# Attention of a second block on Trainium2: logits with keys on the rows instead of transposed probabilities

## The chip, the cores and the metric

The kernel runs on one core of a Trainium2 chip. The metric is the device time of one execution in microseconds. TensorE does the matrix products, VectorE (DVE), ScalarE (ACT) and GpSimd (POOL) the rest; SyncE (SP) issues the DMAs.

## The reference, cut to what matters

Two transformer blocks run one after the other on 512 tokens of width 1024. The second has two layers. Each layer projects its input, mixes it in three ways (a Fourier mix, an attention, a gated recurrence called hgrn), multiplies the joined result by `w_out` and ends with a feed-forward. The change concerns this attention: 8 query heads share 2 key heads, the width of a head is 64, and 512 image queries see 256 context keys and 512 image keys. In the first layer 256 context queries see the context keys alone.

```python
def attend(q, k, v):
    s = jnp.einsum('bkgqd,bksd->bkgqs', q, k).astype(jnp.float32) * (HEAD_DIM ** -0.5)
    p = jax.nn.softmax(s, axis=-1).astype(v.dtype)
    return jnp.einsum('bkgqs,bksd->bkgqd', p, v)
```

## The kernel before, in words

All activations lie with features on the 128 rows and tokens along the columns, in buffers called slots of 128 x 512 numbers. Products that need more than one pass are split: a number is held as a rounded part and a remainder, both of type fp32r, which TensorE takes in one pass; plain fp32 takes more. Weights come in raw buffers of 512 KB and are split by ScalarE and VectorE.

Nothing is ordered by hand. Each piece of work is a generator that yields instructions, requests for buffers, or waits for a result (`Fut`). A planner (`Sched`) holds a clock for each engine, gives each instruction a cost (`mmcost` for matmuls), and always emits the instruction that can start earliest; equal ones go by a task's priority. The order found becomes the order of each engine's queue. Some orders are given: `ORDER2` names the order in which the projections of an image layer run: i (values of the recurrence), kv, hq (queries of the recurrence), q0 and q1 (attention queries of pairs 0, 1 and 2, 3), fo (Fourier), g (gate). The first blocks of each layer are four gates of the recurrence. The context stream of the first layer uses `ORDER2C` and runs beside block 1's feed-forward.

The attention works in pairs of heads, one of either key head: `att2_pair`, four pairs a stream. `stack_q` turns the queries (`turned`) and lays the rounded part and the remainder on the two halves of the 128 rows; `stack_k` does it for the keys. Then each tile of 128 queries runs by itself: `att2_head` makes the logits with queries on the rows, takes the maximum along the columns, the exponential with its sum, divides, and transposes the probabilities by TensorE; `att2_tile` multiplies them by the values, in fp32, with the two heads on the two halves of TensorE's columns. The recurrence (`hgrn`) makes many small products on 64 rows and 32 or 64 columns, each followed by VectorE, GpSimd or ScalarE, and its products cannot start before hq. `out_proj` multiplies the joined result by `w_out` in three parts: part 0 takes three of the eight row blocks (Fourier and pair 0) for the first 256 tokens, part 1 the other five for the same tokens (`OUT2`), part 2 all eight for the last 256 tokens.

PSUM is split by kind: two banks `psm` for the dense products, two `psx` for all else, and two double banks `psd` for logits and the recurrence's small products. When no `psm` is free, a task may take a `psx` instead.

Of the kernel before, what the change touches and what calls it, by code (L numbers as in the profile page):

```python
# [9 lines left out]
F = mybir.dt.float32  # L10
R = mybir.dt.float32r
# [13 lines left out]
HALF = (slice(0, 256), slice(256, 512))  # L25

# [123 lines left out]
ORDER2 = ("i", "kv", "hq", "q0", "fo", "q1", "g")  # L150
# [101 lines left out]
class Alloc:  # L252


    __slots__ = ("kind", "dt", "n")

    def __init__(s, kind, dt=F, n=1):
        s.kind, s.dt, s.n = kind, dt, n
# [177 lines left out]
class Sched:  # L436
# [127 lines left out]
    def run(s):  # L564
        while s.tasks:
            best = None
            progress = False
            for t in list(s.tasks):
                while t.pend is not None:
# [7 lines left out]
                    if isinstance(p, Alloc):  # L577
# [3 lines left out]
                        if len(s.freel[kind]) < p.n + ahead + (ROOM.get(t.name.rstrip("0123456789"), 0) if kind == "slot" else 0):  # L581
                            kind = s.SPARE.get(kind)
# [41 lines left out]
class Kernel:  # L624
    def __init__(s, ctx, tc, A, out, dbg=None):
# [8 lines left out]
            "sm": (sb, [P, 8]), "pr": (sb, [P, 768]), "psm": (pp, [P, T]), "psx": (pp, [P, T]), "psd": (pp, [P, 2 * T]),  # L634
            "tka": (None, None), "tko": (None, None),
        }, {"slot": SLOTS, "raw": 4, "rawc": 2, "wu": 3, "at": 2, "sm": 24, "pr": 4, "psm": 2, "psx": 2, "psd": 2, "tka": 3, "tko": 2})
# [138 lines left out]
    def stack_q(s, q, n, turn=False):  # L775
# [7 lines left out]
        if turn:  # L783
            q = yield from s.turned(q, n)
# [10 lines left out]
    def stack_k(s, kf, n, fut, turn=False):  # L795

        k = yield kf
# [7 lines left out]
        for h in range(2):  # L805
            hi, lo = t[2 * h], t[2 * h + 1]
            own, other = (slice(0, 64), slice(64, P)) if h == 0 else (slice(64, P), slice(0, 64))
# [3 lines left out]
            yield DMA(lo[other].bitcast(F), lo[own].bitcast(F))  # L811
# [1147 lines left out]
    def att2_head(s, i, q, keys, h, fut):  # L1959
        m = yield Alloc("sm")  # L1960
        w = sum(wk for _, wk in keys)
        S = yield Alloc("psd")
        c, mms = 0, []
        for K, wk in keys:
            for j in range(2):
                mms.append((S[:, c:c + wk], q[h][:, i * P:(i + 1) * P], K[h][j], j == 0, j == 1))
            c += wk
        yield PE(*mms)
        yield V("tensor_reduce", m[:, 0:1], S[:, :w], mybir.AxisListType.X, ALU.max, negate=True)
        pr = yield Alloc("pr")  # L1970
        yield ACT("activation", pr[:, :w], S[:, :w], AF.Exp, bias=m[:, 0:1], accum_out=m[:, 1:2])
        s.free(S)
        yield V("reciprocal", m[:, 2:3], m[:, 1:2])
        yield alt(V("tensor_scalar", pr[:, :w], pr[:, :w], m[:, 2:3], None, ALU.mult),
                  G("tensor_tensor", pr[:, :w], pr[:, :w], m[:, 2:3].to_broadcast([P, w]), ALU.mult))
        s.free(m)
        pts = []
        for c0 in range(0, w, T):
            ww = min(T, w - c0)
            pt = yield from s.ps()  # L1980
            yield PE(*[("T", pt[:, c * P:(c + 1) * P], pr[:, c0 + c * P:c0 + (c + 1) * P], s.c["ident"])
                       for c in range(ww // P)])
            t = yield from s.slot(T if ww > TC else TC)
            yield copy_any(t[:, :ww], pt[:, :ww])
            s.free(pt)
            pts += [(t, c) for c in range(ww // P)]
        s.free(pr)
        fut.set(pts)

    def att2_tile(s, i, q, keys, vals, mix, done):  # L1990

        fs = [Fut(), Fut()]
        for h in range(2):
            s.spawn(s.att2_head(i, q, keys, h, fs[h]), 1, "att2h")
        pts = yield from gather(fs)
        mms = []
        nt = len(vals)
        o = yield from s.ps()
        for c in range(nt):
            for h in range(2):  # L2000
                t, cc = pts[h][c]
                mms.append((o[64 * h:64 * h + 64, :P], vals[c][:, 64 * h:64 * h + 64],
                            t[:, cc * P:(cc + 1) * P], c == 0, c == nt - 1, (0, 64 * h)))
        yield PE(*mms)
        for h in range(2):
            s.free(*[t for t, c in pts[h] if c == 0])
        yield from s.split_into(mix, i, o[:, :P])
        s.free(o)
        done.set()

    def att2_pair(s, qf, nq, keysf, valsf, fut, futh=None):
        tok = yield Alloc("tko")
        q0 = yield qf
        q = yield from s.stack_q(q0, nq, True)
# [7 lines left out]
        o = yield from s.pair_mix(nq)  # L2022
        dones = []
        for i in range(nq // P):
            d = Fut()
            dones.append(d)

            def run(i=i, d=d):
                tk = yield Alloc("tka")
                yield from s.att2_tile(i, q, keys, vals, o, d)  # L2030
                s.free(tk)

            s.spawn(run(), 1 + i // 2 * LATE, f"att2_{i}")
        for i, d in enumerate(dones):
            yield d
            if futh is not None and i % 2:
                futh[i // 2].set(o)
        s.free_stack(*q)
        s.free(tok)
        fut.set(o)  # L2040
# [502 lines left out]
    def layer(s, L, adaf, cs=None):  # L2543
# [186 lines left out]
SLOTS = 65  # L2730
# [26 lines left out]
```

## Time and profile before

| | us |
|---|---|
| median of 3 runs | 2281.55 (2280.36 to 2285.49) |
| the profiled execution | 2282.2 |
| its span, first to last instruction | 2280.1 |

A row of the profile holds times in microseconds, or nanoseconds where it says so. PE is TensorE's matmuls, PEld its weight loads, which overlap them. The lengths of matmuls overlap too, since a matmul's record lasts until its last result is out; how fast TensorE works is read from start to start. A plain fp32 matmul stands in the trace as two records. A granted clock of 1.00 is 2.4 GHz.

### The profile page before, as it was taken

How to read it: one execution, taken by the hardware profiler on the slowest of the kernel's cores; microseconds unless marked ns; L12 is line 12 of the kernel's file. 1: busy time of each engine (PE TensorE's matmuls, PEld its weight loads, DVE VectorE, ACT ScalarE, POOL GpSimd, SP SyncE). 2: the span in 40 equal slices, each digit the busy share in tenths (PEclk: the TensorE clock that was granted, in tenths of full speed). 3: DMA queues.
4: the chain of work that ended last, by engine and by line, in shares of the span. 5: the costliest groups of instructions: out<-in, count | busy, mean ns of one | idle time of the engine just before them, and what ended most of it. 6: DMA issues, size and time to landing. Idle time of an engine off the chain costs nothing.

```text
span 2280.1 us, 42611 instructions
## 1 busy us (share of the span) xinstructions
PE 2222.6 (97%) x17065; PEld 1930.2 (85%) x17065; DVE 1559.9 (68%) x3665; ACT 918.6 (40%) x1679; POOL 214.3 (9%) x286
## 2 busy tenths in 40 slices
PE   8999999999999989999999999999989999999998
PEld 6877987888887978799888888889978889888887
DVE  6878877797888678798765433556768776444445
ACT  5455645442224436664212111124536655222223
POOL 0010014110000061110000000000153100000000
PEclk9999999999999989999999999999999999999999
DMA  5455444434444611234433212333221223222223
GB/s 185 145 152 171 167 155 131 144 130 162 147 153 150 199 61 48 93 115 146 148 128 123 102 65 86 126 130 125 105 80 39 75 74 131 93 101 93 99 96 111
DMA packets 92118, 272.72 MB, mean 120 GB/s; under 512 B 10944, under 2 KB 20952, under 8 KB 91920
## 3 DMA queue, kind: packets, MB, share of 16 engines
q1 hardware_dynamic: 91920, 269.99, 35.4%
q8 instruction: 135, 2.21, 0.4%
q14 instruction: 63, 0.52, 0.1%
HBM read 253.66 MB, written 7.38 MB: 114 GB/s over the span
## 4 chain that ended last, share of the span: by engine, by line
PE 87%; DVE 8%; ACT 2%; issue 2%; DMA 1%; POOL 0%; SPq 0%; DVEq 0%; ACTq 0%; POOLq 0%
PE psm L543 67%; PE psx L543 17%; DVE slot L543 6%; PE psd L543 3%; DVE wu L543 2%; ACT slot L543 1%; ACT wu L543 1%; POOL slot L543 0%; DVE sm L543 0%; DMA raw<-w1in 0%; DMA slot<-ctx 0%; DMA slot<-x 0%; DVE at L543 0%; DMA slot<-slot 0%; DMA rawc<-w2in 0%
## 5 line engine op out<-in xcount | busy, mean ns | idle before, releaser
L543 PE MATMUL psm<-slot,wu 128*128 128x256 f32 (+1 forms) x8415 | 1547.3, 342 | 11.7 <-DVE slot L543 9.9
L543 PEld LDWEIGHTS psm<-slot,wu 128*128 128x128 f32 x8415 | 1310.1, 190 | 194.8 <-DVE slot L543 13.6
L543 ACT CAST wu<-raw 128x1024 fp32r<-128x1024 f32 (+1 forms) x325 | 340.5, 1048 | 879.0 <-PE psm L543 499.0
L543 DVE TENSOR_TENSOR wu<-raw,wu 128x1024 fp32r<-128x1024 f32 (+1 forms) x325 | 413.6, 1273 | 198.6 <-ACT wu L543 192.4
L543 DVE CUSTOM_DVE_ANT_0 slot<-rawc,slot 128x256 f32<-128x256 f32 x640 | 273.2, 427 | 97.9 <-DMA rawc<-wada 87.9
L543 POOL TENSOR_TENSOR slot<-slot,slot 128x128 f32<-128x128 f32 (+2 forms) x196 | 133.8, 710 | 875.7 <-DVE slot L543 732.8
L543 DVE TENSOR_TENSOR slot<-slot,slot 128x256 f32<-128x256 f32 (+6 forms) x318 | 179.7, 571 | 12.3 <-ACT slot L543 9.4
L543 PE MATMUL psm<-wu,slot 128*128 128x256 f32 x1344 | 187.2, 289 | 0.3 <-DVE slot L543 0.3
L543 DVE SCALAR_TENSOR_TENSOR slot<-psm,mods,slot 128x256 f32<-128x256 f32 (+1 forms) x189 | 108.1, 572 | 104.5 <-PE psm L543 103.3
L543 DVE TENSOR_TENSOR slot<-slot,psm 128x512 f32<-128x512 f32 (+1 forms) x200 | 117.7, 595 | 81.3 <-PE psm L543 76.5
L543 PEld LDWEIGHTS psm<-wu,slot 128*128 128x128 f32 x1344 | 168.5, 192 | 4.6 <-issue 2.1
L543 PE MATMUL psx<-slot,wu 128*128 128x512 f32 (+1 forms) x849 | 160.9, 344 | 0.4 <-DVE wu L543 0.4
L543 PE MATMUL psd<-slot,slot 64*32 64x32 f32 (+6 forms) x3584 | 128.3, 220 | 23.4 <-DVE slot L543 10.1
L543 PEld LDWEIGHTS psx<-slot,wu 128*128 128x128 f32 x849 | 134.1, 190 | 18.3 <-DVE wu L543 0.8
L543 PEld LDWEIGHTS psd<-slot,slot 64*32 64x32 f32 (+4 forms) x3584 | 95.9, 119 | 55.6 <-POOL slot L543 23.2
L543 PE MATMUL psx<-slot,slot 128*64 128x128 f32 (+6 forms) x1554 | 122.3, 284 | 2.1 <-DVE slot L543 2.1
L543 PEld LDWEIGHTS psx<-slot,slot 128*64 128x64 f32 (+4 forms) x1554 | 92.3, 142 | 26.6 <-issue 11.9
L543 ACT CAST slot<-slot 128x512 fp32r<-128x512 f32 (+3 forms) x142 | 79.5, 561 | 73.8 <-DVE slot L543 53.4
L543 ACT COPY slot<-psx 128x256 f32<-128x256 f32 (+4 forms) x192 | 78.9, 419 | 74.9 <-PE psx L543 65.9
L543 ACT ACTIVATE slot<-slot 128x256 f32<-128x256 f32 (+1 forms) x150 | 64.9, 456 | 35.0 <-DVE slot L543 31.2
L543 DVE SCALAR_TENSOR_TENSOR slot<-slot,mods,slot 128x256 fp32r<-128x256 f32 (+2 forms) x152 | 72.5, 516 | 4.6 <-ACT slot L543 4.5
L543 ACT ACTIVATE pr<-psd,sm 128x768 f32<-128x768 f32 (+1 forms) x80 | 65.3, 818 | 17.8 <-DVE sm L543 17.2
(100 smaller groups left out, 1365.0 us busy)
## 6 DMA issues: line engine op xcount, KB each, us to landing
rawc<-wada SPq DMA_DIRECT2D x96, 512.0 KB, 4.5
raw<-w2gu SPq DMA_DIRECT2D x88, 512.0 KB, 3.3
raw<-w1ff SPq DMA_DIRECT2D x64, 512.0 KB, 3.3
raw<-w2da SPq DMA_DIRECT2D x56, 512.0 KB, 3.3
raw<-w2in SPq DMA_DIRECT2D x36, 512.0 KB, 3.7
raw<-w2out SPq DMA_DIRECT2D x24, 512.0 KB, 3.3
raw<-w1in SPq DMA_DIRECT2D x23, 512.0 KB, 3.6
rawc<-w2in SPq DMA_DIRECT2D x18, 512.0 KB, 3.4
```

The lines of the kernel that those rows point to most:

```text
L543: r = getattr(eng, fn)(*a, **k)
```

## The change

The logits are made twice. `att2_max` makes them once from the rounded parts alone, with queries on the rows, on 64 rows for each head, only to take the maxima. These are turned by small fp32 products with the identity, and the row goes into a free row of a second query operand (`qm`); the second key operand has a 1 in that row. `att2_exp` then makes the full logits, less their maxima, with the keys on the rows and all queries of the stream in the columns, and takes the exponential. Its result goes into the product with the values without a transpose. The sums over keys are made by adding the exponentials of the key tiles and one product with ones; the division is by logarithm and exponential, once for a pair. `stack_q2` lays out two operands for each head. `ORDER2` changes, the half results (`futh`) come together at the end of a pair, the projection by `w_out` no longer takes `psx` banks, and the planner's cost of an fp32r matmul goes by its rows.

```diff
-ORDER2 = ("i", "kv", "hq", "q0", "fo", "q1", "g")
+ORDER2 = ("kv", "q0", "i", "q1", "hq", "fo", "g")
...
     if rhs.dtype == R:
-        return max(107 if m > 64 else 60, n / 2.4) + (2 if n > TC else 4)
+        return (max(107 if m > 64 else 60, n / 2.4) + (2 if n > TC else 4)) * lhsT.shape[0] / P
...
-        }, {"slot": SLOTS, "raw": 4, "rawc": 2, "wu": 3, "at": 2, "sm": 24, "pr": 4, "psm": 2, "psx": 2, "psd": 2, "tka": 3, "tko": 2})
+        }, {"slot": SLOTS, "raw": 4, "rawc": 2, "wu": 3, "at": 2, "sm": 24, "psm": 2, "psx": 2, "psd": 2, "tka": 3, "tko": 2, "tkp": 1, "tkq": 4})
...
-    def stack_q(s, q, n, turn=False):
+    def stack_q2(s, q, n):
+        if n == T:
+            a, b, c, d, x = yield Alloc("slot", R, 5)
...
+        q = yield from s.turned(q, n)
+        for y, h in ((a, 0), (b, 1)):
+            own = OWN[h]
+            yield ACT("copy", y[own], q[own, :n])
+            yield V("tensor_tensor", x[own], q[own, :n], y[own], ALU.subtract)
+        s.free(q)
+        for y, z, h in ((a, c, 0), (b, d, 1)):
+            own, other = OWN[h], OWN[1 - h]
+            yield DMA(y[other].bitcast(F), x[own].bitcast(F))
+            yield DMA(z[own].bitcast(F), y[own].bitcast(F))
+            yield DMA(z[other].bitcast(F), x[own].bitcast(F))
+        s.free(x)
+        return (a, b), (c, d)
...
             yield DMA(hi[other].bitcast(F), hi[own].bitcast(F))
-            yield DMA(lo[other].bitcast(F), lo[own].bitcast(F))
+            if turn:
+                yield V("memset", lo[other].bitcast(F), 0.0)
+                yield V("memset", lo[other.start:other.start + 1].bitcast(F), 1.0)
+            else:
+                yield DMA(lo[other].bitcast(F), lo[own].bitcast(F))
...
-                ps = yield Alloc("psm")
+                ps = yield Alloc("psm", spare=False)
...
-    def att2_head(s, i, q, keys, h, fut):
...
+    def att2_max(s, i, q, keys, nm, j, fut):
         w = sum(wk for _, wk in keys)
+        Ss = yield Alloc("psd", F, 2)
         c, mms = 0, []
         for K, wk in keys:
+            for h in range(2):
+                own = OWN[h]
+                mms.append((Ss[h][:, c:c + wk], q[h][own, i * P:(i + 1) * P], K[h][0][own], True, True, (64 * h, 0)))
             c += wk
         yield PE(*mms)
+        for h in range(2):
+            yield V("tensor_reduce", nm[:, j + h:j + h + 1], Ss[h][:, :w], mybir.AxisListType.X, ALU.max, negate=True)
+            s.free(Ss[h])
+        fut.set()
+
+    def att2_exp(s, K, c, qs, qm, nq, fut):
+        S = yield Alloc("psd")
+        mms = []
+        for h in range(2):
+            for j, q in enumerate((qs, qm)):
+                mms.append((S[:, T * h:T * h + nq], K[h][j][:, c * P:(c + 1) * P], q[h], j == 0, j == 1))
+        yield PE(*mms)
+        pr = yield Alloc("slot", F, 2)
+        for h in range(2):
+            yield ACT("activation", pr[h][:, :nq], S[:, T * h:T * h + nq], AF.Exp)
         s.free(S)
...
-    def att2_tile(s, i, q, keys, vals, mix, done):
...
     def att2_pair(s, qf, nq, keysf, valsf, fut, futh=None):
-        tok = yield Alloc("tko")
+        tok = yield Alloc("tkq")
         q0 = yield qf
-        q = yield from s.stack_q(q0, nq, True)
+        qs, qm = yield from s.stack_q2(q0, nq)
...
+        for i in range(nt):
+            s.spawn(s.att2_max(i, qs, keys, nm, 2 * i, got[i]), 1, "att2m")
+        yield from gather(got)
+        ps = yield from s.ps()
+        yield PE(*[(ps[64 - 64 * h:65 - 64 * h, i * P:(i + 1) * P], nm[:, 2 * i + h:2 * i + h + 1], s.c["ident"], True, True,
+                    (0, 64 - 64 * h)) for i in range(nt) for h in range(2)])
+        for h in range(2):
+            row = slice(64 - 64 * h, 65 - 64 * h)
+            yield copy_any(qm[h][row], ps[row, :nq])
+        s.free(ps, nm)
+        tkp = yield Alloc("tkp")
+        tiles = [(K, c) for K, w in keys for c in range(w // P)]
...
+        s.spawn(logits(), 1, "att2e")
+        o = yield from s.ps()
+        n = len(tiles)
+        acc = None
+        for c, f in enumerate(prs):
+            pr = yield f
+            yield PE(*[(o[64 * h:64 * h + 64, :nq], vals[c][:, 64 * h:64 * h + 64], pr[h][:, :nq], c == 0, c == n - 1,
+                        (0, 64 * h)) for h in range(2)])
+            if acc is None:
+                acc = pr
+                continue
+            for h in range(2):
+                x, z = acc[h][:, :nq], pr[h][:, :nq]
+                yield alt(G("tensor_tensor", x, x, z, ALU.add), V("tensor_tensor", x, x, z, ALU.add))
+            s.free(*pr)
+        den = yield from s.ps()
+        yield PE(*[(den[64 * h:64 * h + 64, :nq], s.c["ones"][:, :64], acc[h][:, :nq], True, True, (0, 64 * h))
+                   for h in range(2)])
+        s.free(*acc)
+        r = yield from s.slot(nq)
+        yield ACT("activation", r[:, :nq], den[:, :nq], AF.Ln)
+        s.free(den, tkp)
+        yield ACT("activation", r[:, :nq], r[:, :nq], AF.Exp, scale=-1.0)
+        yield V("tensor_tensor", r[:, :nq], o[:, :nq], r[:, :nq], ALU.mult)
...
+        mix = yield from s.pair_mix(nq)
+        yield ACT("copy", mix[0][:, :nq], r[:, :nq])
+        yield V("tensor_tensor", mix[1][:, :nq], r[:, :nq], mix[0][:, :nq], ALU.subtract)
...
+        for f in futh or ():
+            f.set(mix)
+        fut.set(mix)
...
-            s.spawn(normfc(), 0.5, "normfc")
+            s.spawn(normfc(), 2.5, "normfc")
...
-SLOTS = 65
+SLOTS = 71
...
-LATE = 0.5
```

## Rows read from the trace of the kernel before

**Rows 1.** The profile page: span, busy time of each engine with its share and instructions, and the shares of the chain that ended last.

```profile
span 2280.1 us, 42611 instructions
...
PE 2222.6 (97%) x17065; PEld 1930.2 (85%) x17065; DVE 1559.9 (68%) x3665; ACT 918.6 (40%) x1679; POOL 214.3 (9%) x286
...
PE 87%; DVE 8%; ACT 2%; issue 2%; DMA 1%; POOL 0%; SPq 0%; DVEq 0%; ACTq 0%; POOLq 0%
```

**Rows 2.** Windows, one row for each stretch of the second block's layers: start and end, length, busy us (instructions) of each engine, granted clock of TensorE, DMA share and GB/s.

```profile
760.00:800.00 40.00, 40.00 (x250) 36.27 (x249) 20.90 (x43) 14.74 (x28) 0.00 (x0) 1.00 0.58 193
800.00:870.00 70.00, 60.97 (x1267) 49.82 (x1265) 55.28 (x133) 32.15 (x78) 47.31 (x71) 0.90 0.17 55
870.00:1005.00 135.00, 131.14 (x1164) 113.91 (x1163) 110.28 (x221) 92.51 (x202) 14.93 (x11) 1.00 0.23 72
1005.00:1075.00 70.00, 70.00 (x585) 69.33 (x584) 61.91 (x172) 35.88 (x60) 0.00 (x0) 1.00 0.51 172
...
1640.00:1675.00 35.00, 35.00 (x304) 34.26 (x304) 10.95 (x29) 10.88 (x20) 0.00 (x0) 1.00 0.19 66
1675.00:1735.00 60.00, 50.49 (x1205) 40.29 (x1204) 50.97 (x124) 26.79 (x69) 46.67 (x70) 0.94 0.17 56
1735.00:1865.00 130.00, 126.81 (x1126) 110.11 (x1126) 102.03 (x199) 84.79 (x180) 10.54 (x8) 1.00 0.19 62
```

**Rows 3.** TensorE in order of time, where dense projections run back to back: start us, length us, engine, line, operation, out<-in, shape, count.

```profile
769.76 12.21 PE L543 MATMUL psm<-slot,wu 128*128 128x512 f32 x53
781.80 3.04 PE L543 MATMUL psm<-wu,slot 128*128 128x256 f32 x24
784.67 3.04 PE L543 MATMUL psx<-wu,slot 128*128 128x256 f32 x24
```

**Rows 4.** The same view in the attention: logits (`psd`), transposes of probabilities (`psx<-c_ident,pr`).

```profile
887.70 0.94 PE L543 MATMUL psd<-slot,slot 128*128 128x512 f32 x4
888.48 0.38 PE L543 MATMUL psx<-c_ident,pr 128*128 128x128 f32 x2
...
889.40 0.82 PE L543 MATMUL psx<-c_ident,pr 128*128 128x128 f32 x6
889.97 1.31 PE L543 MATMUL psm<-wu,slot 128*128 128x256 f32 x9
```

**Rows 5.** The same view around products of probabilities and values (`128*64`), from three places.

```profile
984.24 0.52 PE L543 MATMUL psm<-slot,wu 128*128 128x256 f32 x3
984.69 1.53 PE L543 MATMUL psx<-slot,slot 128*64 128x128 f32 x24
986.15 0.62 PE L543 MATMUL psm<-slot,wu 128*128 128x256 f32 x3
986.61 0.60 PE L543 MATMUL psx<-c_ident,pr 128*128 128x128 f32 x4
...
1816.76 1.02 PE L543 MATMUL psx<-slot,c_bones 128*128 128x512 f32 x2
1817.71 1.53 PE L543 MATMUL psx<-slot,slot 128*64 128x128 f32 x24
...
1864.69 2.84 PE L543 MATMUL psx<-slot,slot 128*64 128x128 f32 x48
1867.46 0.74 PE L543 MATMUL psm<-slot,wu 128*128 128x256 f32 x4
```

**Rows 6.** The same view in the recurrence: blocks of small matmuls on 64 rows (`64*32`) between dense matmuls.

```profile
816.98 0.97 PE L543 MATMUL psm<-slot,wu 128*128 128x512 f32 x3
817.88 0.39 PE L543 MATMUL psd<-slot,slot 64*32 64x32 f32 x32
818.20 0.96 PE L543 MATMUL psm<-slot,wu 128*128 128x512 f32 x3
819.09 0.36 PE L543 MATMUL psd<-slot,slot 64*32 64x32 f32 x32
```

**Rows 7.** Groups of instructions over the whole run, kept apart by shape: count | busy us, mean ns of one | idle of the engine ahead of them.

```profile
L543 DVE TENSOR_REDUCE sm<-psd 128x1 f32<-128x768 f32 x64 | 60.0, 950 | 5.1 <-PE psd L543 4.7
L543 ACT ACTIVATE pr<-psd,sm 128x768 f32<-128x768 f32 x64 | 57.8, 904 | 11.9 <-DVE sm L543 11.3
L543 DVE TENSOR_TENSOR slot<-slot,slot 128x512 fp32r<-128x512 f32 x82 | 55.9, 683 | 0.7 <-ACT slot L543 0.7
...
L543 DVE TENSOR_SCALAR pr<-pr,sm 128x768 f32<-128x768 f32 x53 | 33.7, 636 | 1.6
...
L543 POOL TENSOR_TENSOR slot<-slot,slot 128x512 f32<-128x512 f32 x17 | 26.0, 1537 | 112.3 <-DVE slot L543 46.8 <-issue 42.3 <-ACT slot L543 17.4
...
L543 DVE TENSOR_TENSOR slot<-slot,slot 128x512 f32<-128x512 f32 x31 | 22.5, 738 | 0.6 <-ACT slot L543 0.6
...
L543 ACT ACTIVATE slot<-slot 128x512 f32<-128x512 f32 x31 | 19.3, 627 | 10.3 <-DVE slot L543 10.1
...
L543 ACT ACTIVATE slot<-psx 128x512 f32<-128x512 f32 x10 | 6.0, 596 | 13.4 <-PE psx L543 13.4
```

**Rows 8.** DMA issues: out<-in, queue, count, KB each, median us from issue to landing.

```profile
slot<-slot SPq DMA_DIRECT2D x60, 128.0 KB, 3.5
```

**Rows 9.** Waits from 800 to 870 us: engine and what it waited for: us in total, times, longest us.

```profile
PEld psd L543 <- POOL slot L543: 8.7, 11, 1.7
```

**Rows 10.** A window of 5 us inside the recurrence, columns as in rows 2.

```profile
845.00:850.00 5.00, 4.18 (x89) 3.37 (x90) 5.00 (x17) 1.61 (x5) 2.97 (x7) 0.50 0.01 3
```

More of the change, by code (lines that the diff above doesn't have):

```diff
@@ L252, with __init__ @@
 class Alloc:
-    __slots__ = ("kind", "dt", "n")
-    def __init__(s, kind, dt=F, n=1):
-        s.kind, s.dt, s.n = kind, dt, n
+    __slots__ = ("kind", "dt", "n", "spare")
+    def __init__(s, kind, dt=F, n=1, spare=True):
+        s.kind, s.dt, s.n, s.spare = kind, dt, n, spare
 def is_ap(a):
@@ L581, in run @@
                         if len(s.freel[kind]) < p.n + ahead + (ROOM.get(t.name.rstrip("0123456789"), 0) if kind == "slot" else 0):
-                            kind = s.SPARE.get(kind)
+                            kind = s.SPARE.get(kind) if p.spare else None
                             if kind is None or len(s.freel[kind]) < 2:
@@ L633, in __init__ @@
             "slot": (sb, [P, T]), "raw": (sb, [P, 1024]), "rawc": (sb, [P, 1024]), "wu": (sb, [P, 2048]), "at": (sb, [P, 8, P]),
-            "sm": (sb, [P, 8]), "pr": (sb, [P, 768]), "psm": (pp, [P, T]), "psx": (pp, [P, T]), "psd": (pp, [P, 2 * T]),
-            "tka": (None, None), "tko": (None, None),
-        }, {"slot": SLOTS, "raw": 4, "rawc": 2, "wu": 3, "at": 2, "sm": 24, "pr": 4, "psm": 2, "psx": 2, "psd": 2, "tka": 3, "tko": 2})
+            "sm": (sb, [P, 8]), "psm": (pp, [P, T]), "psx": (pp, [P, T]), "psd": (pp, [P, 2 * T]),
+            "tka": (None, None), "tko": (None, None), "tkp": (None, None), "tkq": (None, None),
+        }, {"slot": SLOTS, "raw": 4, "rawc": 2, "wu": 3, "at": 2, "sm": 24, "psm": 2, "psx": 2, "psd": 2, "tka": 3, "tko": 2, "tkp": 1, "tkq": 4})
         s.spawn = s.q.spawn
@@ L782, in stack_q @@
             x = x[:, :n]
-        if turn:
-            q = yield from s.turned(q, n)
         yield ACT("copy", a[:64], q[:64, :n])
@@ L806, in stack_k @@
             hi, lo = t[2 * h], t[2 * h + 1]
-            own, other = (slice(0, 64), slice(64, P)) if h == 0 else (slice(64, P), slice(0, 64))
+            own, other = OWN[h], OWN[1 - h]
             yield ACT("copy", hi[own], k[own, :n])
@@ L1976, in att2_head @@
[L1976 to L1987, printed above, removed]
@@ L1988, in att2_head @@
-        fut.set(pts)
-    def att2_tile(s, i, q, keys, vals, mix, done):
[L1992 to L2009, printed above, removed]
+        for h in range(2):
+            yield V("tensor_reduce", nm[:, j + h:j + h + 1], Ss[h][:, :w], mybir.AxisListType.X, ALU.max, negate=True)
+            s.free(Ss[h])
@@ L2021, in att2_pair @@
             vals += [t[:, b * P:(b + 1) * P] for b in range(nb)]
[L2022 to L2037, printed above, removed]
@@ L2038, in att2_pair @@
-        s.free_stack(*q)
+        nt = nq // P
+        nm = yield Alloc("sm")
+        got = [Fut() for _ in range(nt)]
+        for i in range(nt):
[7 more added lines that the diff above has]
+            yield copy_any(qm[h][row], ps[row, :nq])
@@ new lines, in att2_pair, with logits @@
+        s.free(ps, nm)
+        tkp = yield Alloc("tkp")
+        tiles = [(K, c) for K, w in keys for c in range(w // P)]
+        prs = [Fut() for _ in tiles]
+        def logits():
+            for (K, c), f in zip(tiles, prs):
+                yield from s.att2_exp(K, c, qs, qm, nq, f)
+        s.spawn(logits(), 1, "att2e")
[13 more added lines that the diff above has]
+            s.free(*pr)
```

21 lines of the change are left out of this document (10 added, 11 removed).

## The prediction

> **What bounds the kernel now.** I read the page first [rows 1]. TensorE is busy for 2222.6 us of a span of 2280.1; VectorE stands at 68%, ScalarE at 40%, and 87% of the chain that ended last lies on TensorE. So only two things move the end: TensorE's own work, and the places where TensorE stands still or slow. Next I cut both layers of the second block into stages by windows [rows 2]. In layer 0 (layer 1 in brackets) they are: the projections of i, kv and hq, 760 to 800 (1640 to 1675), TensorE full, VectorE only 20.9 of 40 us (10.9 of 35); the start of the recurrence, 800 to 870 (1675 to 1735), TensorE busy 60.97 of 70 us (50.49 of 60) at a granted clock of 0.90 (0.94), VectorE at 79% (85%); the attention, 870 to 1005 (1735 to 1865), TensorE 131.14 of 135 us (126.81 of 130); the output projection from 1005 on, no gap at all. The attention that the change rewrites is bound by TensorE's pace, so what VectorE and ScalarE save there is worth nothing by itself. What can be won beside TensorE's work is the stretch before it. In the recurrence TensorE idles 9.0 + 9.5 us, and the clock takes 7.0 + 3.6 us more (0.10 x 70 and 0.06 x 60): 29 us. The attention stretches add 3.9 + 3.2. All losses together are 36 us.
>
> **What TensorE's work costs.** Its records overlap, so I read starts, not lengths. A dense fp32r matmul takes 0.120 us for 256 columns (24 in 2.87 us) and 0.227 for 512 (53 in 12.04) [rows 3]. One head of a query tile (512 image keys, 256 context keys) costs now: logits 0.78 us and six transposes 0.57, 1.35 together (887.70 to 888.48, 889.40 to 889.97) [rows 4]; less four matmuls at the dense pace (0.69), a transpose is 0.109. Probabilities times values of a tile, both heads, is 24 records in 1.46 us (984.69 to 986.15), but 48 in 2.77: 0.0545 a record, 1.31 a tile, and 0.15 for the block itself [rows 5]. The block also costs around it: three dense matmuls take 0.45 us ahead of it and 0.46 behind it (984.24, 986.15), not 0.36. So each block that uses half of the array's columns costs 0.15 + 0.09 + 0.10 = 0.34 us beyond its work. The recurrence's blocks with 64 rows behave alike: three 512-column matmuls between two of them take 0.89 to 0.90 us, not 0.68 [rows 6].
>
> The Trainium skill, "TensorEngine Tiling (Array Packing)", section "Tiling Modes", states that changing the tiling mode drains TensorE. This speaks against the change, which multiplies such blocks; the page gives no price, and the 0.34 us above is this trace's.
>
> **The change on TensorE, per pair of heads in the image stream.** Before: 8 x 1.35 = 10.8; 4 x (1.31 + 0.34) = 6.6; sum 17.4 us. After:
> - Maxima: per query tile 2 heads x (512 + 256) columns at 64 rows. The trace has no such fp32r matmul with all columns. If both row halves run together, 0.35 us a tile; if not, 0.70. The nearest row is the recurrence's: 32 matmuls on 64 rows, of both halves and 32 columns each, start within 0.32 us [rows 6]. I take 0.35: 1.4 us.
> - Maxima turned into a row: 8 fp32 matmuls of 128 columns, two records each at 0.0545: 0.9 us. Below stands nearly nothing, since one output column is far less than 64; above, 8 transposes at 0.109 are the same 0.9.
> - Logits with keys on the rows: 6 key tiles x 4 x 0.227 = 5.45 us.
> - Probabilities times values at 512 columns: four times the columns, 4 records x 0.218 = 0.87 a key tile. Two full-width fp32 matmuls of 512 columns take 0.95 us with a switch behind them, which fits [rows 5]. 6 x 0.87 = 5.2 us, and 0.87 for the denominator.
> - Sum 13.8 us, and the switches: 4 tiles of maxima, 1 row, 6 key tiles, 1 denominator = 12 x 0.34 = 4.1. Total 17.9, 0.5 us more than before. Eight pairs: +4 us.
>
> The removed transposes and the shorter logits are paid back by eight more switches. In the context stream (256 queries and keys, 4 pairs, inside block 1's full feed-forward) a pair costs now, at the same paces, 4 x 0.24 for logits, 8 x 0.109 for transposes and 2 x (8 x 0.0545 + 0.34) for values: 3.4 us. After: 0.24 + 0.44 + 0.96 + 0.87 + 0.44 = 2.95, and 6 switches: 5.0. Four pairs: +6.5 us.
>
> TensorE's work: +10.5 us. Lower end +1: key tiles leave in twos, which drops three switches a pair (one in the context). Upper end +22: the row halves do not overlap. I take +10.5, since two PSUM buffers for the logits (`psd`) let a value block follow about one exponential at a time, with dense work between.
>
> **The other engines.** Removed per image pair: 8 reciprocals, 8 scalings of 768 columns (0.64 us on VectorE), 16 copies of transposes. Kept: 8 maxima at 0.95 us. Added: 10 sums of 512 columns (0.74 us on VectorE, 1.54 on GpSimd), 12 exponentials of 512 columns (about 0.60, by the 512-column activation out of PSUM) for 8 of 0.90, and a tail of a logarithm, an exponential, a product, a cast and a subtraction (0.60 + 0.63 and, by the subtraction, 3 x 0.68: 3.3 us) [rows 7]. Both engines end up with less to do. I count that at nothing: TensorE covers it; without that cover it would be a gain where VectorE binds, in the recurrence. DMAs: stack_q2 issues six for two, 4 x 12 more, and the four key stacks drop eight: +40 on SyncE's queue, 3.5 us to landing each [rows 8]. SyncE waits there for the query split, and weight loads stand behind; four raw buffers cover it, each worth 2.9 us or more of matmuls. The first exponentials wait for those landings, behind the maxima phase, which has 8 x 0.95 us on VectorE. `o` holds one of two `psx` banks through a pair, so dense units lose their spare bank; the attention's own matmuls fill in.
>
> **The moved steps.** kv and q0 come first, so pairs 0 and 1 can run beside i, q1 and hq, where VectorE was half idle [rows 2]. The recurrence needs hq and i and starts some 23 us of dense matmuls later (q0 and q1: 2 x 96 x 0.120). After hq there remain for TensorE: fo and g (11.5 + 10.9), two pairs (36), the first part of the output projection (8 x 9 x 0.120 = 8.6), the Fourier part: 67 us and more, beside the recurrence that took 60 to 70. That can fill the gaps, which came from waits on VectorE's and GpSimd's products in TensorE's in-order queue [rows 9]; the recurrence has as many such waits as before, and now shares VectorE with the maxima. I take a quarter of the 36 us as won (-9). Against it, both halves of a pair's result now come at its end, with the 3.3 us tail: +3 over both layers. Losses: -6.
>
> **Sum.** The profiled execution took 2282.2 us (span 2280.1), 0.7 above the median of 2281.55. 2282.2 + 10.5 - 6 = 2286.7; against the median, 2286. A measurement of this kernel can tell about 0.2% (4.6 us) from no change; the forecast sits at that edge.
>
> **Rivals.**
> - The recurrence is filled (not slower). Its gaps and slow clock nearly vanish, -24 of 36 us: 2281.5 + 10.5 - 24 = 2268. For it: the rich mix after hq, and a clock that fell to 0.50, the lower of its two levels, 1.2 GHz, only where the recurrence's small blocks were most of TensorE's work (845 to 850) [rows 10]. Against it: the same in-order waits. It decides from 15 us won.
> - The recurrence ends late (slower). Output projection part 1 needs both its results for its very first column block. If attention finishes before hq, only 31 us of dense work covers a recurrence of 60 to 70; with VectorE shared I price 10 us exposed per layer: 2281.5 + 10.5 - 6 + 20 = 2306. It decides once the recurrence outlasts part 0 of the output projection.
> - Switches cost nothing: work 13.8 against 16.1 per image pair, 2.95 against 2.7 in the context: -18 + 1; with -6, 2259. Against it: the 0.34 us of [rows 5], seen at nearly every block.
> - The row halves do not overlap: +12, 2298. Against it: the packed starts of [rows 6], though those matmuls are small.
>
> The Trainium skill, "TensorE: Matmul & The Clock Gate", section "Part 3: Packing small matmuls", prices a packed group at one matmul and some 4 ns per tile, which is the third rival's time; the trace agrees within a block, where two records of half the columns take the 0.109 us of one full-width transpose, but not at its edges.
>
> **How the numbers follow.** Forecast 0.40, with its own range 2278 to 2296; filled 0.27; late 0.20; no switch cost 0.06; no overlap 0.07. Faster: 0.27 + 0.06 = 0.33. Same: half of the forecast, 0.20. Slower: 0.20 + 0.20 + 0.07 = 0.47. The range 2262 to 2306 leaves out the no-switch case, the edge of the filled one and half of the late one, 0.2 in all.
>
> **What would show it.** Right: image-pair blocks of 12 per pair, each 0.34 us over its work; maxima of 0.35 us a tile; value blocks of about 1.0 us per key tile; the context stretch of block 1 some 6 us longer. Wrong: value blocks mostly in twos or threes; maxima at 0.7; the recurrence's TensorE gaps below 2 us a layer, or a gap over 8 us just ahead of the output projection's second part.

## The result

The changed kernel takes 2303.91 us (median; 2300.52 to 2306.88), the kernel before, on the same chip, 2283.52 (2280.36 to 2287.1): a ratio of 1.0088 [1.0064, 1.0113], 20 us slower. TensorE's work came out near the forecast, the losses beside it did not.

The page of the kernel after, for [rows 1]:

```profile
span 2298.7 us, 41000 instructions
...
PE 2235.9 (97%) x16329; PEld 1864.5 (81%) x16329; DVE 1551.0 (67%) x3525; ACT 873.1 (38%) x1522; POOL 274.3 (12%) x335
```

TensorE issues 736 matmuls fewer than before and is busy 13.3 us longer; VectorE and ScalarE do less, GpSimd more. To see where the 18.6 us of span lie, I cut both traces at the same amount of dense work: from the 1100th dense matmul to the 2300th (context attention), from the 3200th to the 4600th (layer 0 of the second block) and from the 8000th to the 8950th (layer 1). Windows of the kernel before, columns as in [rows 2]:

```profile
275.59:525.08 249.49, 243.59 (x1937) 205.97 (x1936) 200.47 (x514) 114.85 (x233) 51.29 (x62) 1.00 0.43 143
731.14:1059.69 328.55, 314.29 (x3333) 279.12 (x3332) 261.72 (x574) 187.47 (x379) 62.24 (x82) 0.98 0.34 112
1623.01:1878.48 255.47, 242.77 (x2887) 214.00 (x2885) 187.98 (x402) 137.75 (x301) 59.94 (x84) 0.99 0.20 66
```

And of the kernel after:

```profile
274.93:530.09 255.16, 249.75 (x1936) 204.60 (x1935) 201.06 (x496) 112.23 (x214) 52.73 (x60) 1.00 0.44 147
738.30:1074.13 335.83, 315.56 (x2965) 245.61 (x2964) 250.00 (x475) 165.03 (x307) 85.63 (x107) 0.98 0.34 111
1636.69:1896.45 259.76, 246.51 (x2518) 184.28 (x2517) 185.22 (x343) 116.52 (x234) 90.39 (x108) 0.97 0.23 72
```

Length less TensorE's busy time is idle time; length times (1 - granted clock) is what the slow clock takes; the rest I call work. The stretches grew by 5.7, 7.3 and 4.3 us, 17.2 of the 18.6. Work grew by 6.2, 3.0 and 0.3 (9.5 in all). Idle time and slow clock, the losses, grew in the two layers from 37.2 to 45.5, by 8.3, of which 6.6 are idle time. (The clock is taken with four digits, in the table below too.)

How far these figures carry, two runs of the table below show. e2 has the same matmuls as before in another order, and 5.5 us more work in layer 0: the 3.0 and 0.3 of the layers are not clear of that. The 6.2 of the context are (243.5 to 244.2 in the four kernels with the attention of before there, 249.2 to 249.8 in the five with that of after). e8 has the order of after on every engine in both layers; its idle time there is within 1 us of after's, its slow clock in layer 0 is 11.9 us for 5.1. So in this pair idle time repeats from one execution to another, and slow clock does not.

The pieces of a pair, in TensorE's order of time: the maxima of two tiles with dense work between, those of a third with their row, a place where TensorE waits for VectorE, and two key tiles without dense work between:

```profile
841.46 0.62 PE L544 MATMUL psd<-slot,slot 64*128 64x512 f32 x4
842.01 3.72 PE L544 MATMUL psx<-slot,wu 128*128 128x512 f32 x15
845.65 0.61 PE L544 MATMUL psd<-slot,slot 64*128 64x512 f32 x4
...
848.13 1.07 PE L544 MATMUL psm<-slot,wu 128*128 128x512 f32 x4
849.13 0.61 PE L544 MATMUL psd<-slot,slot 64*128 64x512 f32 x4
849.67 1.04 PE L544 MATMUL psx<-c_ident,sm 128*1 128x128 f32 x16
...
895.15 0.62 PE L544 MATMUL psd<-slot,slot 64*128 64x512 f32 x4
...
896.54 0.96 PE L544 MATMUL psm<-slot,wu 128*128 128x512 f32 x3 [0.17 <-ACT slot L544]
900.32 0.44 PE L544 MATMUL psd<-slot,slot 64*32 64x32 f32 x32 [2.81 <-DVE sm L544]
...
1831.12 1.19 PE L544 MATMUL psd<-slot,slot 128*128 128x512 f32 x4
1832.24 1.08 PE L544 MATMUL psx<-slot,slot 128*64 128x512 f32 x4
1833.25 1.19 PE L544 MATMUL psd<-slot,slot 128*128 128x512 f32 x4
1834.37 1.08 PE L544 MATMUL psx<-slot,slot 128*64 128x512 f32 x4
1835.38 0.82 PE L544 MATMUL psx<-c_ident,sm 128*1 128x128 f32 x12
```

A key tile, logits and values, takes 2.13 us (1831.12 to 1833.25, and again to 1835.38). The forecast was 0.907 for the logits, 0.87 for the values and 0.34 for the switch: 2.12. The maxima of a tile, 2 x 768 columns, take 0.54 us (849.13 to 849.67): 0.35 for columns that run on both row halves at once, and 0.2 for the block itself. The 15 dense matmuls between two such blocks take 3.64 us (842.01 to 845.65), 0.23 more than at the dense pace of [rows 3]: a tile of maxima costs 0.77 us, so its price beyond the columns is 0.42.

At 900.32 a matmul of the recurrence waits 2.81 us for a logits buffer that holds maxima, those of 895.15, which took both. The same stretch on VectorE shows the first reduction (`sm<-psd`) behind three of the recurrence's products and a weight split in its in-order queue, and the second 2.6 us later:

```profile
894.65 2.31 DVE L544 TENSOR_TENSOR wu<-raw,wu 128x1024 fp32r<-128x1024 f32 x1
896.88 2.43 DVE L544 TENSOR_TENSOR slot<-slot,slot 128x128 f32<-128x128 f32 x3
899.23 0.94 DVE L544 TENSOR_REDUCE sm<-psd 128x1 f32<-128x768 f32 x1
...
901.81 0.94 DVE L544 TENSOR_REDUCE sm<-psd 128x1 f32<-128x768 f32 x1
```

Over the whole run, two groups of TensorE's matmuls of the kernel before (busy us, mean ns | idle time ahead of them and what ended it):

```profile
L543 PE MATMUL psd<-slot,slot 64*32 64x32 f32 (+6 forms) x3584 | 128.3, 220 | 23.4 <-DVE slot L543 10.1 <-POOL slot L543 4.2 <-DMA slot<-slot 3.5
L543 PE MATMUL psx<-c_ident,slot 128*128 128x128 f32 x227 | 40.5, 286 | 4.6 <-DVE slot L543 2.5 <-ACT slot L543 1.7
```

The same two groups of the kernel after:

```profile
L544 PE MATMUL psd<-slot,slot 64*32 64x32 f32 (+7 forms) x3664 | 149.4, 225 | 22.9 <-DVE sm L544 7.6 <-POOL slot L544 4.7 <-DVE slot L544 4.2
L544 PE MATMUL psx<-c_ident,slot 128*128 128x128 f32 x227 | 39.7, 282 | 7.8 <-DVE slot L544 6.2 <-ACT slot L544 1.7
```

The idle time ahead of the logits and the recurrence stays at 23 us: waits for VectorE's products fell from 10.1 to 4.2, and waits for the maxima, 7.6 us (5.6 of them ahead of the recurrence), took their place. The turns of the second group (queries, keys and the recurrence's) wait 3.2 us more. New are two waits of 1.84 us at 820.17 and 1.85 us at 1688.31, for the first queries of a layer:

```profile
820.17 0.44 PE L544 MATMUL psx<-c_ident,slot 128*128 128x128 f32 x2 [1.84 <-DVE slot L544]
...
859.88 0.62 PE L544 MATMUL psd<-slot,slot 64*128 64x512 f32 x4
...
862.51 0.35 PE L544 MATMUL psd<-slot,slot 64*32 64x32 f32 x32
...
864.12 1.09 PE L544 MATMUL psd<-slot,slot 128*128 128x512 f32 x4
```

The last three rows show where the pairs lie. Ahead of the recurrence, whose first products stand at 862.51, only maxima run; the first full logits of layer 0 stand at 864.12. In layer 1 the two start together, at 1731.61 and 1732.6. In the kernel before, the recurrence's products on logits buffers had all run (the last at 863.9 and 1730.3) when the first logits came (872.4 and 1738.8), so the two did not meet there.

### The profile page after: what moved, and what is told of

Same layout as the page of the kernel before. It is cut to its first block, busy times and chain, and to the rows that moved or that the text cites. A ratio compares the mean times of both kernels' runs of the same rounds, so it can differ in the third digit from the quotient of the medians.

```text
span 2298.7 us, 41000 instructions
## 1 busy us (share of the span) xinstructions
PE 2235.9 (97%) x16329; PEld 1864.5 (81%) x16329; DVE 1551.0 (67%) x3525; ACT 873.1 (38%) x1522; POOL 274.3 (12%) x335
## 4 chain that ended last, share of the span: by engine, by line
PE 57%; DVE 5%; issue 1%; ACT 1%; POOL 0%; DMA 0%; DVEq 0%; ACTq 0%; POOLq 0%
PE psm L544 43%; PE psx L544 11%; PE psd L544 3%; DVE slot L544 3%; DVE wu L544 1%; ACT slot L544 1%; DVE sm L544 1%; POOL slot L544 0%; ACT wu L544 0%; DVE at L544 0%; DMA raw<-w2outk 0%; DMA slot<-slot 0%; ACT at L544 0%; ACT sm L544 0%; DVEq L2795 0%
## 5 line engine op out<-in xcount | busy, mean ns | idle before, releaser
L544 PE MATMUL psm<-slot,wu 128*128 128x512 f32 (+1 forms) x8490 | 1549.3, 341 | 13.5 <-DVE slot L544 10.5
L544 PEld LDWEIGHTS psm<-slot,wu 128*128 128x128 f32 x8490 | 1314.1, 190 | 213.6 <-issue 21.1
L544 POOL TENSOR_TENSOR slot<-slot,slot 128x128 f32<-128x128 f32 (+2 forms) x264 | 212.9, 828 | 1035.6 <-DVE slot L544 739.1
L544 DVE TENSOR_TENSOR slot<-slot,slot 128x256 f32<-128x256 f32 (+6 forms) x349 | 211.6, 614 | 39.9 <-ACT slot L544 34.4
L544 PEld LDWEIGHTS psd<-slot,slot 64*32 64x32 f32 (+5 forms) x3664 | 97.2, 119 | 98.4 <-issue 49.9
L544 PE MATMUL psd<-slot,slot 64*32 64x32 f32 (+7 forms) x3664 | 149.4, 225 | 22.9 <-DVE sm L544 7.6
L544 PE MATMUL psx<-slot,slot 128*64 128x128 f32 (+10 forms) x946 | 127.8, 365 | 3.7 <-ACT slot L544 1.9
L544 PEld LDWEIGHTS psx<-slot,slot 128*64 128x64 f32 (+4 forms) x946 | 58.9, 142 | 38.3 <-issue 18.0
L544 ACT ACTIVATE slot<-slot 128x256 f32<-128x256 f32 (+1 forms) x162 | 71.2, 462 | 37.2 <-DVE slot L544 32.4
L544 DVE TENSOR_REDUCE sm<-psd 128x1 f32<-128x768 f32 (+1 forms) x80 | 64.7, 843 | 19.3 <-PE psd L544 19.0
L544 ACT ACTIVATE slot<-psm 128x256 f32<-128x256 f32 (+1 forms) x122 | 56.1, 478 | 51.0 <-PE psm L544 50.9
L544 DVE SCALAR_TENSOR_TENSOR slot<-slot,mods,slot 128x256 f32<-128x256 f32 (+2 forms) x152 | 72.2, 511 | 4.3 <-ACT slot L544 4.3
```

What stands on the lines that cost most here:

```text
L544: r = getattr(eng, fn)(*a, **k)
```

## The experiments

Each kernel is timed against the kernel before on the same chip. Work, idle time and slow clock are those of the same stretches in its one profiled execution; for the context its length is given.

| kernel | us | ratio, interval | context | layer 0: work, idle, clock | layer 1: work, idle, clock |
|---|---|---|---|---|---|
| before | 2283.5 | 1 | 249.5 | 307.5, 14.3, 6.8 | 239.4, 12.7, 3.4 |
| after | 2303.9 | 1.0088 [1.0064, 1.0113] | 255.2 | 310.4, 20.3, 5.1 | 239.7, 13.2, 6.8 |
| e1 | 2324.7 | 1.0188 [1.0173, 1.0203] | 254.9 | 311.5, 19.9, 10.2 | 243.0, 20.1, 6.8 |
| e2 | 2306.7 | 1.0108 [1.0094, 1.0122] | 251.1 | 313.0, 23.1, 3.4 | 239.9, 19.7, 10.2 |
| e3 | 2300.4 | 1.0081 [1.0067, 1.0095] | 254.2 | 311.9, 18.5, 1.7 | 240.1, 14.1, 3.4 |
| e4 | 2317.2 | 1.0150 [1.0134, 1.0166] | 254.0 | 306.1, 25.1, 8.5 | 233.9, 21.1, 8.5 |
| e5 | 2293.3 | 1.0041 [1.0026, 1.0056] | 249.7 | 293.4, 22.9, 3.4 | 223.4, 24.6, 15.4 |
| e6 | 2343.6 | 1.0268 [1.0252, 1.0284] | 266.4 | 310.2, 22.9, 8.5 | 236.9, 20.5, 10.2 |
| e7 | 2310.8 | 1.0123 [1.0106, 1.0140] | 261.0 | 309.3, 18.4, 5.1 | 240.2, 15.2, 0.0 |
| e8 | 2299.3 | 1.0072 [1.0057, 1.0087] | 249.2 | 307.7, 21.1, 11.9 | 239.6, 13.5, 6.8 |
| e9 | 2260.5 | 0.9901 [0.9886, 0.9915] | 250.3 | 290.9, 18.8, 8.5 | 223.5, 13.2, 1.7 |
| e10 | 2309.6 | 1.0113 [1.0098, 1.0128] | 255.6 | 307.8, 26.3, 8.5 | 236.5, 15.8, 6.8 |
| e11 | 2300.8 | 1.0070 [1.0053, 1.0088] | 255.0 | 310.2, 16.5, 8.5 | 240.2, 13.9, 3.4 |
| e12 | 2301.7 | 1.0089 [1.0075, 1.0103] | 253.9 | 311.6, 17.9, 1.7 | 237.3, 14.5, 10.2 |

e5 and e9 leave the maxima out. In all others the work columns keep within 7 and 9 us (306 to 313 and 234 to 243), and the losses within 15 and 16 (20 to 35 and 15 to 31).

**The order, undone and alone.** e1 is the kernel after with the order before, e2 the kernel before with the order of after but for hq, which stands ahead of q1:

```diff
-ORDER2 = ("kv", "q0", "i", "q1", "hq", "fo", "g")
+ORDER2 = ("i", "kv", "hq", "q0", "fo", "q1", "g")     # e1, on after
-ORDER2 = ("i", "kv", "hq", "q0", "fo", "q1", "g")
+ORDER2 = ("kv", "q0", "i", "hq", "q1", "fo", "g")     # e2, on before
```

> The changed kernel with the projections in the order of before (i, kv, hq, q0, fo, q1, g); all else as changed. The account of the two traces so far: TensorE's work at full clock grew by about 10 us (6 in the context stream, 3 to 4 in the image layers), and idle time and slow clock in the two layers by about 8 us. Theory A: those 8 us come from the order, since two pairs of the attention now run when the dense projections are used up. Then this kernel takes about 2296 us, and idle time and clock loss of the two layers return to about 36 us. Rival B: they come from the rewritten attention itself (results at the end of a pair, two double banks at once for the maxima). Then it stays at about 2304 us.

> The kernel before with the order kv, q0, i, hq, q1, fo, g, the nearest to the changed order that fits in its buffers (hq stands one place earlier); attention as before. Theory A (the order costs): slower than before by 5 to 8 us. Rival B (the attention costs): within 3 us of before.

Neither number came. On the new attention the old order costs 21 us (2324.7), 12 of them losses in the layers; on the old attention another order costs 24 (2306.7), 19 of them losses. The change's own order does not fit the buffers of the old attention, so no run has that. In these two pairs of runs the order has no worth by itself; each attention did better with its own.

**The maxima on full rows.** The maxima are taken on all 128 rows, so that their blocks switch nothing, but head runs after head:

```diff
-                mms.append((Ss[h][:, c:c + wk], q[h][own, i * P:(i + 1) * P], K[h][0][own], True, True, (64 * h, 0)))
+                mms.append((Ss[h][:, c:c + wk], q[h][:, i * P:(i + 1) * P], K[h][0], True, True))
```

> The changed kernel with the first logits, for the maxima, on all 128 rows (rounded parts and remainders of the queries together) and no tile position. A tile of maxima then costs 2 x (0.227 + 0.118) = 0.69 us of plain work in place of 0.35 of work and 0.34 for the switch. Theory S (each block on part of the array costs 0.34 us): the time does not change, within 3 us of the changed kernel (2304). Rival N (a switch costs nothing): 32 tiles x 0.35 = 11 us more, 2315.

2300.4, 3.5 us less than after, with intervals that overlap. Against after it has another order too: the planner now prices the maxima as in e11 below. With e11 it shares the order on every engine, and the two differ in the form of the maxima alone: 2300.4 and 2300.8. Twice the columns without a switch cost the same as half of them with one (0.69 us a tile by the paces, against 0.77 with the switch above). In the context, where the work is clear, e3 has 1.5 us less of it for 8 tiles (248.3 for 249.8): 0.19 a tile, with 0.12 of columns added, so a switch takes 0.31. That fits the price of 0.34 us; a switch that costs nothing is out.

**Values in blocks of two key tiles.**

```diff
-        for c, f in enumerate(prs):
-            pr = yield f
+        for c0 in range(0, n, 2):
+            cs = range(c0, min(n, c0 + 2))
+            got = yield from gather([prs[c] for c in cs])
```

> The changed kernel with the products of exponentials and values issued for two key tiles at a time, so that a pair has 3 such blocks and not 6 (context stream: 1 and not 2). Theory S: 8 x 3 x 0.34 + 4 x 0.34 = 9.5 us less, 2294. Rival N: 2304, or more, since the first tile of two waits for the second.

Missed: 2317.2. The work did fall, by 4.3 and 5.9 us in the layers; the switches saved should give 8.2, and the context's work fell by 1.6 for a forecast of 1.4. But the losses in the layers rose by 18 us (45.5 to 63.3). That the second key tile of each block has to be waited for is the likely reason; no run isolates it. A value block of e4, two key tiles in 1.86 us where two blocks of after take 1.01 each (1832.24 to 1833.25), and the logits behind it:

```profile
960.62 1.94 PE L544 MATMUL psx<-slot,slot 128*64 128x512 f32 x8
962.48 1.20 PE L544 MATMUL psd<-slot,slot 128*128 128x512 f32 x4
```

**Without maxima.** The whole phase of maxima and its row goes:

```diff
-        for i in range(nt):
-            s.spawn(s.att2_max(i, qs, keys, nm, 2 * i, got[i]), 1, "att2m")
...
-            yield ACT("activation", pr[h][:, :nq], S[:, T * h:T * h + nq], AF.Exp)
+            yield ACT("activation", pr[h][:, :nq], S[:, T * h:T * h + nq], AF.Exp, scale=1.0 / 128)
```

> The changed kernel with the maxima and their row left out of the second block's attention (no maxima matmuls, no reductions, no row; the exponentials are scaled by 1/128 so that they stay finite, and their values are others). The work that goes is, by the rows after, 8 pairs x (4 x 0.69 + 1.24) = 32 us in the layers and 4.9 us in the context. Theory M: the 8 us of new losses in the two layers are the maxima phase itself, TensorE held by the logits' PSUM pair until VectorE has reduced it. Then the losses go back to 37 us or less, and the time is 2304 - 37 - 8 = 2259 us or below. Theory F: the losses are a matter of how the order of units and the attention's form fit together, and no one wait carries them. Then they need not fall: 2304 - 37 = 2267 us or above.

2293.3, so not the 2259 of the first theory: some 40 us of work went (17.1 + 16.3 + 6.3), and only 10.6 us of time. In layer 0 the losses stayed, in layer 1 they doubled (20.1 to 40.0). Windows of e5 in layer 1:

```profile
1690.00:1730.00 40.00, 40.00 (x195) 22.75 (x194) 15.65 (x23) 20.22 (x36) 15.51 (x12) 1.00 0.08 27
1730.00:1800.00 70.00, 60.49 (x1221) 42.55 (x1220) 57.56 (x124) 30.56 (x64) 53.22 (x76) 0.95 0.22 63
1800.00:1862.00 62.00, 49.83 (x256) 27.29 (x255) 24.01 (x54) 25.75 (x51) 7.29 (x5) 0.82 0.15 51
```

Two pairs run from 1690 to 1725 with no small matmul of the recurrence beside them; the recurrence follows (1221 matmuls of all kinds in 70 us); and from 1800 on little is left to fill with: TensorE stands for 12.2 of 62 us, in gaps of at most 3.2, at a clock of 0.82. The attention was done too early, and the recurrence's end, the Fourier part and the wait of the output projection lie bare.

**Without maxima, hq one place earlier.** The recurrence can start before q1 is projected:

```diff
-ORDER2 = ("kv", "q0", "i", "q1", "hq", "fo", "g")
+ORDER2 = ("kv", "q0", "i", "hq", "q1", "fo", "g")
```

> The kernel without the maxima and their row (as in e5_no_maxima, exponentials scaled by 1/128), with hq ahead of q1: kv, q0, i, hq, q1, fo, g. In e5 both first pairs were finished before the recurrence began (attention 1690 to 1728, recurrence from 1730), and the recurrence's end, the out-projection's wait for it and 12 us of gaps and a low clock stood bare at the end of layer 1 (1810 to 1862). Theory R (what counts is whether the attention still lies beside the recurrence): begun 23 us of dense matmuls earlier, the recurrence ends under cover, the losses of e5 in layer 1 (40 us) fall by 12 us or more, and the time is 2293 - 12 = 2281 us or less. Theory C (each order of units falls anew, with no rule): 2281 to 2305.

2260.5, 33 us less than e5 by one moved step and no work. Windows of e9 in layer 1:

```profile
1690.00:1730.00 40.00, 35.51 (x503) 16.30 (x502) 26.88 (x41) 19.02 (x38) 32.26 (x35) 1.00 0.04 15
1730.00:1800.00 70.00, 64.05 (x983) 52.54 (x985) 52.60 (x123) 33.48 (x75) 35.85 (x56) 0.98 0.29 89
1800.00:1840.00 40.00, 40.00 (x216) 22.00 (x217) 19.31 (x27) 23.83 (x41) 13.91 (x10) 1.00 0.13 43
```

The recurrence has begun by 1730 (503 matmuls against 195), and the end of the layer has no gap: losses of 14.9 us for 40.0. For this pair of kernels it shows what the losses hang on: dense and attention work must still be there when the recurrence has its gaps.

**With maxima, hq one place earlier.** The same edit on the kernel after.

> The changed kernel with hq ahead of q1 (kv, q0, i, hq, q1, fo, g), else as after; the same order on the attention of before was the run with the order alone. In the changed kernel the recurrence ends at about 1850, with attention still to do until 1875, so it is not bare. Theory R: nothing to win at the end of the layer; pair 1 comes later instead, as with the old order; 2304 us or above, up to the old order's 2325. If the hold-up is the recurrence's end all the same: below 2295.

2309.6, 5.7 more than after, as expected. In the kernel after the maxima hold the attention back, so that its last pairs still lie beside the recurrence's end (in layer 1 its last output product stands at 1846.8, the attention runs to 1877); there is nothing bare to cover. With this order the maxima cost 49 us (2309.6 - 2260.5), for some 37 of work (16.9 + 13.0 in the layers, 6.8 in the context).

**One logits buffer at a time.** e10 with the maxima taken head by head on full rows, each from one `psd` buffer instead of both at once:

```diff
-        Ss = yield Alloc("psd", F, 2)
...
         for h in range(2):
+            S = yield Alloc("psd")
...
+            yield PE(*mms)
+            yield V("tensor_reduce", nm[:, j + h:j + h + 1], S[:, :w], mybir.AxisListType.X, ALU.max, negate=True)
+            s.free(S)
```

> The changed kernel with hq ahead of q1 (as e10_hq_earlier, 2309.6 us), and the maxima taken one head at a time on all 128 rows, so that each asks for one of the two PSUM buffers of logits where it asked for both at once; full rows alone cost nothing in e3_full_rows. In e10 TensorE stood 7.1 us in gaps that the reductions of the maxima ended, and with this order the maxima cost 49 us (2309.6 against 2260.5 without them), 12 more than their 37 us of work. Theory H (the 12 us come of holding both buffers): most comes back, 2302 us or less. Against it (VectorE's 0.95 us a reduction and the order set it, not the buffers): 2306 to 2313.

2301.7, within the first theory's 2302: 7.9 less by the medians; by the ratios 0.0024, or 5.5 us. In e10 TensorE stands where both buffers are with VectorE:

```profile
866.91 0.61 PE L544 MATMUL psd<-slot,slot 64*128 64x512 f32 x4
868.57 0.49 PE L544 MATMUL psd<-slot,slot 64*128 64x512 f32 x1 [1.05 <-DVE sm L544]
870.76 0.61 PE L544 MATMUL psd<-slot,slot 64*128 64x512 f32 x3 [1.70 <-DVE sm L544]
```

The gaps over 0.25 us that a reduction of maxima ended sum to 7.1 us in the layers of e10 and to 2.4 in e12. Layer 0 lost 15.2 us less, layer 1 2.1 more; idle time alone fell by 9.7. So 4.7 us of idle time were waits for the reductions, which speaks for the double hold as a cause of the losses. That all 6 to 8 us come of it, of the 12 that the maxima cost beyond their work in this order, is not shown: e12 has full rows too, and the planner gave it another order.

**The context as before.** Only the image stream has the new attention.

```diff
-            s.spawn(s.att2_pair(st.qf[j], TC, [(st.ks, TC)], [(st.vf, 2)], mix[2 + j]), 2, f"attc{j}")
+            s.spawn(s.att2_pair_c(st.qf[j], TC, [(st.ks, TC)], [(st.vf, 2)], mix[2 + j]), 2, f"attc{j}")   # the functions of before
```

> The changed kernel with the attention of the context stream as before (query tiles, transposed probabilities, the same keys), the image stream's as after. By the rows after, the context stretch then costs 5.7 us less, of which 6.2 are work. If what was lost in the context lasts to the end: 2304 - 6 = 2298 us. If the later units make the place good (that stretch has dense work in reserve, so work moved there is work either way, but idle time could come back): 2300 to 2304.

2299.3, 4.6 less by the medians, between the two expectations, with intervals that overlap. The window of the context stretch in e8:

```profile
277.68:526.92 249.24, 243.68 (x1937) 205.77 (x1935) 201.88 (x521) 114.88 (x234) 49.94 (x59) 1.00 0.43 147
```

TensorE's 243.68 us of busy time are those of before (243.59), 6.1 below after. How much of that lasts to the end is not settled: in the profiled execution layer 0, in the order of after, took 340.8 us for 335.8, with 11.9 us of slow clock for 5.1.

**The planner's prices.** e6 (on after) and e7 (on before) tell the planner the switch; e11 (on after) undoes the price that the change gave to 64-row matmuls:

```diff
+    op.cost += 340 * any(len(m) > 5 for m in mms)                      # e6, e7
...
-        return (max(107 if m > 64 else 60, n / 2.4) + (2 if n > TC else 4)) * lhsT.shape[0] / P
+        return max(107 if m > 64 else 60, n / 2.4) + (2 if n > TC else 4)     # e11
```

> The changed kernel, with the planner's price of every block on half or part of the array raised by 340 ns, the price read from the trace of before; the instructions are the same, their order follows the new price. Theory L: the planner takes a block as free at its edges, falls behind the chip by 0.34 us with each, and so issues blocks whose operands are later than it believes; with the true price the losses fall from 45 us to below 30, and the time is 2304 - 15 = 2289 us or less. Theory F (fit, no one cause): the losses change by some us of either sign, 2295 to 2315.

> The kernel before with the same raised price. Theory L: its 37 us of losses fall too, to below 27; 2283 - 10 = 2273 us or less. Theory F: 2275 to 2295, of either sign.

> The changed kernel with one line of the change undone: the planner prices a matmul on 64 of 128 rows as one on 128 again (the price fell to half). No instruction is other, only the order in which the planner issues them can be. Theory C (the losses follow from small differences in the order): the time moves by 5 us or more in either sense, though the work is the same. Theory D (the losses come from the change's structure): within 5 us of 2304.

The theory that the planner is late by the price of its switches fell: 2343.6 and 2310.8, 40 and 27 us slower and outside the rival's ranges too, mostly before the second block's layers begin (the context stretch alone grows by 11 us in both). e11 gave the layers another order and moved the time by 3 us, with intervals that overlap: not every change of order costs.

## Why the prediction was right, and where it was wrong

The forecast was 2286, its own range 2278 to 2296, the whole range to 2306, with slower as the likeliest sign. The sign is right, and 2303.9 lies near the upper end; the likeliest case's range was missed by 8 us. That the time lies in the whole range at all is luck: its upper part stands for the rival "ends late", which is not what happened.

- **The price of a block, 0.34 us: right.** A key tile takes 2.13 us for 2.12; a block of maxima costs 0.42, a switch in the context 0.31 (e3 against e11). The Trainium skill, "TensorEngine Tiling (Array Packing)", section "Tiling Modes", states the drain at a change of mode; the trace agrees in that each such block costs about 0.34 us. The rival in which switches cost nothing (2259) is out.
- **The row halves run together: right inside the block.** 0.54 us for the maxima of a tile, of which 0.35 are columns. The Trainium skill, "TensorE: Matmul & The Clock Gate", section "Part 3: Packing small matmuls", prices such a group at one matmul and some 4 ns for each further tile; the trace agrees on the starts (849.126 and 849.130 us for the two heads), and the 0.2 us of the block itself stands beside it.
- **TensorE's work, +10.5 us: right for the context, near for the images.** 9.5 measured: context 6.2 for 6.5, images 3.3 for 4, a difference that the order alone can make (e2). The lower bound (value blocks in twos) did not happen by itself: 46 of 47 value blocks in the layers hold one key tile. The upper one (no overlap) did not either.
- **Losses, -6: wrong, +8.3.** This step failed. It took a quarter of the 36 us as won (-9) because two pairs move beside i, q1 and hq, and dense work stays for the recurrence. The pairs did not move: ahead of the recurrence only maxima run (862.51 and 864.12 above), and the maxima phase holds the full logits back: without it, in e5, those of layer 1 start at 1689.8, well ahead of the recurrence's products on logits buffers at 1734.5. The idle time ahead of the recurrence's own matmuls in the two layers is 16.1 us before and 16.9 after: nothing was won. The step named the maxima's share of VectorE, and went on to price only the attention's late end (+3). It did not see that `att2_max` holds both logits buffers, which the recurrence needs too, until VectorE's in-order queue comes to the reductions. Those waits are 7.6 us, 5.6 ahead of the recurrence; before, the reductions of 950 ns [rows 7] held one buffer each and came when the recurrence's products on these buffers were done. The turns, of which the queries' come right behind their projection now, add 3.2 us. Of the 3 us for the tail at most 1.6 are to be seen: gaps of 0.38 us behind the last pair of layer 0 (1009.14) and of 0.39 and 0.80 behind that of layer 1 (1882.43, 1883.61).
- **The rival "ends late", 2306: its time came, its mechanism not.** A gap of over 8 us ahead of the output projection is not in the trace of after, where the largest behind the attention is 1.36 us. The recurrence's end lies bare only in e5, where the maxima are gone, and there as 12.2 us of short gaps; e9 closes them. **"Filled", 2268,** did not come either: by their releasers, the recurrence's waits in after are for the maxima and for products on VectorE and GpSimd (7.6, 4.2 and 4.7 us ahead of the logits and the recurrence).

What is shown: the price of a block (e3 against e11, in one order), the context's work, that the recurrence waits for buffers which the maxima hold, and that losses follow where the attention lies beside the recurrence (e5 against e9). That the hold explains all that e12 won is argued. What stays open: e3 and e11, which share an order, lose 38 and 42 us in the layers, near the 37 of before, and still end at 2300. What they save there goes again in the feed-forward behind layer 0 (5.3 and 3.5 us longer than in after, from the 4600th to the 8000th dense matmul); why, no run tells. No kernel tried with the full computation beat the kernel before.

## What to carry to other kernels

Count blocks on part of the array like instructions: here each costs 0.3 to 0.4 us beyond its columns, whether it holds 4 records or 24, and replacing long passes by many short blocks can eat the columns saved. Where TensorE's queue is in order, ask of each new phase which shared buffers it holds while it waits for another engine, and who queues for them. Look in the trace whether a moved step really went where the order puts it. Work that covers a recurrence's gaps is worth its place only as long as it is still there when the gaps come: removing 40 us of work gave 11, and moving one step gave 33.

## What the runs showed of the hardware

A block of 64-row fp32r matmuls runs both row halves together: 2 x 768 columns in 0.54 us, against 0.69 for the same columns at the dense pace of [rows 3]; the two heads' matmuls start 4 ns apart (849.126 and 849.130). The granted clock fell again where TensorE had gaps: from 0.95 to 0.82 in e5 (1800 to 1862, 12.2 us idle), and it stood at 1.00 in the same part of the layer in e9, which has no gap. One order can meet different clocks: layer 0 of after and of e8, the same on every engine, lost 5.1 and 11.9 us to it.
